# Two heads at a time in the dilated attention, and joined values in the mixer's

## The chip, the cores and the metric

The kernel runs on one core of a Trainium2 chip. Its metric is the device time of one execution in microseconds. TensorE (PE) multiplies, VectorE (DVE) and ScalarE (ACT) do the elementwise work, GpSimd (POOL) a few additions, and SyncE (SP) issues nearly all DMAs.

## What is computed

Two transformer blocks follow one another on 256 tokens of width 1024, in fp32. The first is FFN, a hybrid mixer (causal latent attention with 8 heads, and a gated convolution) and FFN. The second is a mixer of two attentions (branch A with 8 heads of 128, and branch B), an FFN and a gated embedding. The two places that matter here, cut down:

```python
def causal_mla_attention(...):            # mixer of block one, per head of 64 (+32 rotary)
    sc = (q_nope @ k_nope.T + q_rope @ k_rope.T) * scale      # 96 deep
    p = softmax(where(key <= query, sc, -inf))
    return p @ v                                              # 64 wide

def mixer_b(q, k, v, rel_bias):           # branch B of block two: 3 dilations x 4 heads of 64
    for g, (window, dilation) in enumerate(((128, 1), (512, 4), (2048, 16))):
        o, lse = dilated_group(...)       # banded softmax(q @ k.T + bias) @ v
    wts = softmax(stack(lses))            # over the three dilations
    return sum(wts * stack(outs))         # 4 heads of 64
```

## The kernel before

The activations lie transposed, features on partitions and tokens in the free dimension. A weight strip (256 columns of a matrix with 1024 rows) is loaded by SP into one of three `raw` buffers, ScalarE casts it to fp32r (`hi`), VectorE computes the rest (`lo`), and each product is three fp32r matmuls (lines 150 to 152): hi by hi, hi by lo, lo by hi. `gemm` runs 24 of them into half a bank of PSUM.

Attention is done in plain fp32. The generator `_stages` (line 38) works on the heads as a pipeline of three stages, which are called last stage first in each round: scores, then a turn (transposes of the probabilities on PE, and a copy out of PSUM by ScalarE), then values. `_interleave` (line 28) alternates these with steps of a projection. So the source has an order of its own, but each engine's order is fixed when the program is built and is not the source's: in the trace, later projections stand between steps that the source has closer together.

In the mixer of block one (from line 742) a head's scores are 96 rows deep. The values of an even head write partitions 0 to 63 of a bank `bo`, those of the odd head after it partitions 64 to 127, each two products (lines 774 and 776); after the odd one the bank is split into `oaH` and `oaL`. The projection work beside it is `gl`, later `y`.

In branch B (lines 1092 to 1137) an item is one head and one half of the queries, eight in all. The three dilations share one softmax over 512 columns: 256 keys of dilation 1, 128 each of dilations 4 and 16. Scores (line 1103) are three products over the 64 rows on which this head lies: partitions 0 to 63 or 64 to 127 of `qkB`. `bias_tile` (line 896) loads a bias tile from DRAM with two DMAs on SP, and GpSimd adds the masks to the near part, which `bias_near` has loaded once a head with four DMAs. VectorE adds the bias and takes the maximum (line 1108), ScalarE takes the exponential, VectorE scales by the reciprocal sum (line 1113). Four transposes follow (line 176), a copy (line 1121), and four products of values (line 1132) into the 64 partitions of `bob` that belong to the head. After two heads `bob` is copied, reordered and split. Beside it run the projection of branch A (`ya`, in `out_a`) and, after that, the gates (`gab`, `yb`, line 1183 on), whose `sg` takes a buffer of the tag `z`.

PSUM has two pools of four banks: `bankA` (scores, transposes, values) and `bankB` (projections).

Of the kernel before, what the change touches and what calls it, by code (L numbers as in the profile page):

```python
# [8 lines left out]
F32 = mybir.dt.float32  # L9
# [3 lines left out]
AF = mybir.ActivationFunctionType  # L13
ALU = mybir.AluOpType
# [13 lines left out]
def _interleave(a, b, na=1, nb=1):  # L28
    a, b = iter(a), iter(b)
    live_a = live_b = True  # L30
    while live_a or live_b:
        for _ in range(na):
            if live_a:
                try:
                    next(a)
                except StopIteration:
                    live_a = False
        for _ in range(nb):
            if live_b:
                try:  # L40
                    next(b)
                except StopIteration:
                    live_b = False


def _stages(n, stages, also):

    out = [None] * len(stages)
    for i in range(n + len(stages) - 1):
        if i in also:  # L50
            also[i]()
            yield
        new = list(out)
        for k in range(len(stages) - 1, -1, -1):
            if 0 <= i - k < n:
                new[k] = stages[k](*(out[k - 1] if k else (i,)))
                yield
        out = new
# [3 lines left out]
def tile_two_blocks(ctx: ExitStack, tc: tile.TileContext, t: dict, out: bass.AP):  # L62
# [11 lines left out]
    def bankA(name):  # L74
        return psA.tile([P, 512], F32, tag="acc", name=name)

    def bankB(name):
        return psB.tile([P, 512], F32, tag="ps", name=name)
# [4 lines left out]
    def tab(*args, **kw):  # L83
        if not last_table:
            last_table.append(act.activation(*args, **kw).ins)
        else:
            with tc.issue_after(last_table[0]):
                last_table[0] = act.activation(*args, **kw).ins  # L88
# [82 lines left out]
    def hilo(src, hi, lo):  # L171
        act.copy(hi, src)  # L172
        vec.tensor_tensor(out=lo, in0=src, in1=hi.bitcast(F32), op=ALU.subtract)  # L173

    def tr(dst, src, n=P):
        pe.transpose(out=dst, in_=src, identity=ident[:n, :n])
# [412 lines left out]
    def mixer_one(px, tmp2):  # L589
# [36 lines left out]
        def latent():  # L626
# [110 lines left out]
            o_attn.extend((oaH, oaL))  # L737
            scale = 96.0 ** -0.5
            regions = ((0, P), (P, 384))
            bo = {}  # L740

            def scores(hd):
                bs = bankA("bs")
# [17 lines left out]
            def turn_p(hd, sm):  # L761
                bt = bankA("bt")
                for i in range(3):
                    tr(bt[:, i * P:(i + 1) * P], sm[:, i * P:(i + 1) * P])
                pT = tmp2.tile([P, 384], F32, tag="pT", name="pT")
                act.copy(pT, bt[:, :384])
                return hd, pT

            def values(hd, pT):
                j = hd % 2  # L770
                if j == 0:
                    bo[0] = bankA("bo")
                o = bo[0][j * 64:j * 64 + 64, :]
                pe.matmul(o[:, 0:T], lhsT=vN[:, 0, hd * 64:hd * 64 + 64], rhs=pT[:, 0:T], start=True, stop=False,
                          skip_group_check=True)
                pe.matmul(o[:, P:T], lhsT=vN[:, 1, hd * 64:hd * 64 + 64], rhs=pT[:, T:384], start=False, stop=True,
                          skip_group_check=True)
                if j:
                    hilo(bo[0][:, :T], oaH[:, hd // 2, :], oaL[:, hd // 2, :])

            yield from _stages(8, (scores, turn_p, values), {2: lambda: (turn(nq, qT, "mq", 2), turn(nq, qT, "mq", 3))})

# [99 lines left out]

    def bias_near(px, j):

        stg = px.tile([P, 80], F32, tag="bias_s", name="bias_s", bufs=2)
        for rr in range(2):
            p0 = rr * 64

            for g, dst, su in ((1, stg[p0:p0 + 64, 0:64], (16 * 512 - 1, 512 - 4)),
                               (2, stg[p0:p0 + 64, 64:80], (16 * 512, 512 - 1))):  # L890
                row0 = ((4 * g + j) * P + p0) * 512
                sync.dma_start(out=dst, in_=bass.AP(bias_d.tensor, bias_d.offset + row0 + 256,
                                                    [[su[0], 4], [su[1], 16], [1, dst.shape[1]]]))
        return stg

    def bias_tile(px, j, qt, stg):

        bt = px.tile([P, 512], F32, tag="bias", name="bias", bufs=2)
        for rr in range(2):
            p0 = rr * 64  # L900
            row0 = (j * P + p0) * 512
            sync.dma_start(out=bt[p0:p0 + 64, 0:256],
                           in_=bass.AP(bias_d.tensor, bias_d.offset + row0 + 256 - 2 * qt - rr,
                                       [[16 * 512 - 4, 4], [512 - 16, 16], [1, 256]]))
        for m, a, n, o, so in ((m1, 2, 64, 256, 0), (m2, 8, 16, 384, 64)):
            pool.tensor_tensor(out=bt[:, o:o + P].rearrange("p (a b) -> p a b", a=a),
                               in0=m.rearrange("p (a b) -> p a b", a=a),
                               in1=stg[:, so:so + n].unsqueeze(1).to_broadcast([P, a, n]), op=ALU.add)
        return bt
# [5 lines left out]
    def mixer_two(px, tmp2):  # L915
# [17 lines left out]
        gg = tmp2.tile([P, 2, P], F32, tag="pT", name="gg")  # L933
        act.dma_start(out=gg[:, 0, :], in_=row_bc(t["q_norm_g_2"], P))
        act.dma_start(out=gg[:, 1, :], in_=row_bc(t["k_norm_g_2"], P))
        rtab = [px.tile([P, 2, 256], F32, tag="bias", name="rtab", bufs=2) for _ in range(2)]
        blk = lambda z: z.rearrange("p a (f s n) -> p a f s n", f=2, s=2)
        for i in range(2):
            g1 = gg[:, i:i + 1, :].to_broadcast([P, 2, P])
# [150 lines left out]
        bo_b, stage_b, ya = {}, {}, []  # L1090

        def scores_b(i):
            j, qt = divmod(i, 2)
            pr_, jj = divmod(j, 2)
            lo_, hi_ = jj * 64, jj * 64 + 64
            if qt == 0:
                stage_b[0] = bias_near(px, j)
            bias = bias_tile(px, j, qt, stage_b[0])
            bs = bankA("bs")
            qs = slice(qt * P, (qt + 1) * P)  # L1100
            for g in range(3):
                dst, ks = ((bs[:, 0:256], slice(0, T)), (bs[:, 256:384], qs), (bs[:, 384:512], qs))[g]
                pe.matmul(dst, lhsT=qB[lo_:hi_, 2 * g + pr_, qs], rhs=kB[lo_:hi_, 2 * g + pr_, ks], start=True, stop=True)
            sm = tmp2.tile([P, 512], F32, tag="sm", name="sm", bufs=3)
            mx = tmp.tile([P, 1], F32, tag="mx1", name="mx1")
            nb = tmp.tile([P, 1], F32, tag="nb1", name="nb1")
            se = tmp.tile([P, 1], F32, tag="se1", name="se1")
            vec.tensor_tensor_reduce(out=sm, in0=bs, in1=bias, scale=1.0, scalar=-3e38,
                                     op0=ALU.add, op1=ALU.max, accum_out=mx)
            vec.tensor_scalar_mul(nb, mx, -1.0)  # L1110
            tab(sm, sm, AF.Exp, bias=nb, accum_out=se)
            vec.reciprocal(se, se)
            vec.tensor_scalar_mul(sm, sm, se)
            return i, sm

        def turn_b(i, sm):
            bt = bankA("bt")
            for c in range(4):
                tr(bt[:, c * P:(c + 1) * P], sm[:, c * P:(c + 1) * P])
            pT = tmp2.tile([P, 512], F32, tag="pT", name="pT")  # L1120
            act.copy(pT, bt)
            return i, pT

        def values_b_of(i, pT):
            j, qt = divmod(i, 2)
            pr_, jj = divmod(j, 2)
            if i % 4 == 0:
                bo_b[0] = bankA("bob")
            bo = bo_b[0]
            for c in range(4):  # L1130
                v = vB[(0, 0, 1, 2)[c]][:, (0, 1, qt, qt)[c], j * 64:(j + 1) * 64]
                pe.matmul(bo[jj * 64:jj * 64 + 64, qt * P:(qt + 1) * P], lhsT=v, rhs=pT[:, c * P:(c + 1) * P],
                          start=c == 0, stop=c == 3, skip_group_check=True)
            if i % 4 == 3:
                fl = tmp.tile([P, T], F32, tag="nu", name="ob")
                act.copy(v16(fl), o16(bo[:, :T]))
                hilo(fl, obH[:, pr_, :], obL[:, pr_, :])

        def out_a():
            ya.append(px.tile([P, 8, T], F32, tag="qA", name="ya"))  # L1140
            for s in range(4):
                w = cols(t["w_out_a_2"][0], s * 256, 256)
                b = bankB("ya")
                for j in range(2):
                    gemm(b[:, j * T:(j + 1) * T], w, j * P, (oaH, oaL), KD)
                    yield
                vec.tensor_copy(flat(ya[0][:, 2 * s:2 * s + 2, :]), b)
# [22 lines left out]
                drain(q[0])  # L1170
        B = qkv_b()
        _interleave(chain(_stages(8, (scores_a, turn_a, values_a_of), {1: lambda: drain(q[1]), 3: lambda: drain(q[2]), 5: lambda: drain(q[3])})), B, 2, 1)
        _interleave(_stages(8, (scores_b, turn_b, values_b_of), {}), out_a())
        rb = rbs[0]
        wob = cols(t["w_out_b_2"][0], 0, 1024)
        mgH = px.tile([P, KD, T], F32R, tag="oAH", name="mgH2")
# [178 lines left out]
```

## Time and profile before

| | |
|---|---|
| median of 3 runs | 1050.9 us (1048.54 to 1056.88) |
| the profiled execution's own time | 1048.57 us |
| its span, first to last instruction | 1046.8 us |
| mean granted TensorE clock | 0.995 |
| PE busy | 1018.4 us (97%) |
| DVE busy | 741.7 us (71%) |
| ACT busy | 557.3 us (53%) |

Busy time is a share of the span; matmuls are pipelined, so the busy time of PE counts their overlaps once, and its rate is read from the distance between starts. PEld is the weight load of TensorE, which has rows of its own.

### The profile page before, as it was taken

How to read it: one execution, taken by the hardware profiler on the slowest of the kernel's cores; microseconds unless marked ns; L12 is line 12 of the kernel's file. 1: busy time of each engine (PE TensorE's matmuls, PEld its weight loads, DVE VectorE, ACT ScalarE, POOL GpSimd, SP SyncE). 2: the span in 40 equal slices, each digit the busy share in tenths (PEclk: the TensorE clock that was granted, in tenths of full speed). 3: DMA queues.
4: the chain of work that ended last, by engine and by line, in shares of the span. 5: the costliest groups of instructions: out<-in, count | busy, mean ns of one | idle time of the engine just before them, and what ended most of it. 6: DMA issues, size and time to landing. Idle time of an engine off the chain costs nothing.

```text
span 1046.8 us, 20303 instructions
## 1 busy us (share of the span) xinstructions
PE 1018.4 (97%) x8332; PEld 984.3 (94%) x8332; DVE 741.7 (71%) x1414; ACT 557.3 (53%) x1036; POOL 34.9 (3%) x47
## 2 busy tenths in 40 slices
PE   6999999999999999999999999999999999999996
PEld 3799999999989998999999999999899999999996
DVE  4789998657967998964545689656467776555565
ACT  5564554447656455643444555544456665445453
POOL 0000000010000011000000100001100100000010
PEclk9999999999999999999999999999999999999998
DMA  9899999425754987986554344445335885555311
GB/s 346 287 373 337 304 343 367 142 87 173 214 178 151 290 262 271 343 274 212 170 193 153 112 128 155 135 135 165 96 123 188 267 285 186 183 187 195 121 62 41
DMA packets 161301, 215.41 MB, mean 206 GB/s; under 512 B 6206, under 2 KB 129877, under 8 KB 161080
## 3 DMA queue, kind: packets, MB, share of 16 engines
q1 hardware_dynamic: 159346, 212.58, 61.4%
q10 hardware_dynamic: 1862, 1.53, 0.5%
q8 instruction: 65, 1.06, 0.4%
q14 instruction: 28, 0.23, 0.1%
HBM read 210.63 MB, written 3.47 MB: 205 GB/s over the span
## 4 chain that ended last, share of the span: by engine, by line
PE 82%; DVE 9%; ACT 3%; DMA 3%; issue 1%; POOL 0%; SPq 0%; DVEq 0%; ACTq 0%; POOLq 0%
PE gu L150 8%; PE gu L152 8%; PE gu L151 8%; PE acc L150 7%; PE acc L151 7%; PE acc L152 6%; DVE lo L140 3%; PE u L152 2%; PE u L150 2%; PE u L151 2%; PE gab L150 1%; DMA ada<-in_w_ada_dram 1%; ACT hi L139 1%; PE gab L152 1%; PE gab L151 1%
## 5 line engine op out<-in xcount | busy, mean ns | idle before, releaser
L140 DVE TENSOR_TENSOR lo<-raw,hi 128x512 fp32r<-128x512 f32 (+2 forms) x454 | 395.7, 903 | 102.9 <-ACT hi L139 101.7
L139 ACT CAST hi<-raw 128x512 fp32r<-128x512 f32 (+2 forms) x454 | 337.1, 786 | 222.3 <-PE acc L151 81.6
L150 PE MATMUL gu<-hh,hi 128*128 128x256 f32 x704 | 198.8, 283 | 0.0
L152 PE MATMUL gu<-hh,lo 128*128 128x256 f32 x704 | 197.6, 281 | 0.0
L151 PE MATMUL gu<-hl,hi 128*128 128x256 f32 x704 | 196.8, 280 | 0.0
L150 PE MATMUL acc<-mh,hi 128*128 128x256 f32 x608 | 170.2, 282 | 2.3 <-ACT mh L172 2.3
L151 PE MATMUL acc<-ml,hi 128*128 128x256 f32 x608 | 170.8, 281 | 0.0
L152 PE MATMUL acc<-mh,lo 128*128 128x256 f32 x608 | 170.2, 280 | 0.0
L151 PEld LDWEIGHTS gu<-hl,hi 128*128 128x128 f32 x704 | 133.0, 189 | 0.6 <-issue 0.5
L150 PEld LDWEIGHTS gu<-hh,hi 128*128 128x128 f32 x704 | 132.9, 189 | 0.6 <-issue 0.5
L152 PEld LDWEIGHTS gu<-hh,lo 128*128 128x128 f32 x704 | 132.8, 189 | 0.1
L150 PEld LDWEIGHTS acc<-mh,hi 128*128 128x128 f32 x608 | 114.0, 188 | 2.8 <-ACT mh L172 2.8
L151 PEld LDWEIGHTS acc<-ml,hi 128*128 128x128 f32 x608 | 114.5, 188 | 0.2 <-DVE ml L173 0.2
L152 PEld LDWEIGHTS acc<-mh,lo 128*128 128x128 f32 x608 | 114.7, 189 | 0.0
L267 DVE SCALAR_TENSOR_TENSOR ada_acc<-ada,c_act,ada_acc 128x512 f32<-128x512 f32 x98 | 73.6, 751 | 2.3 <-DMA ada<-in_w_ada_dram 0.6
L150 PE MATMUL u<-hh,hi 128*128 128x256 f32 x256 | 71.6, 280 | 0.0
L151 PE MATMUL u<-hl,hi 128*128 128x256 f32 x256 | 71.6, 280 | 0.0
L152 PE MATMUL u<-hh,lo 128*128 128x256 f32 x256 | 71.5, 279 | 0.0
L88 ACT ACTIVATE s<-gu 128x256 f32<-128x256 f32 x44 | 16.7, 382 | 75.2 <-PE gu L152 75.2
L331 POOL TENSOR_TENSOR ssum<-ssum,sq 128x256 f32<-128x256 f32 x25 | 23.3, 931 | 813.6 <-ACT sq L329 812.6
L151 PEld LDWEIGHTS u<-hl,hi 128*128 128x128 f32 x256 | 48.1, 188 | 0.2 <-DVE hl L376 0.2
L150 PEld LDWEIGHTS u<-hh,hi 128*128 128x128 f32 x256 | 48.1, 188 | 0.0
(379 smaller groups left out, 2221.9 us busy)
## 6 DMA issues: line engine op xcount, KB each, us to landing
raw<-in_ffn_w_dram SPq DMA_DIRECT2D x64, 1024.0 KB
raw<-in_w_in_dram SPq DMA_DIRECT2D x37, 1024.0 KB
raw<-in_w_ff_dram SPq DMA_DIRECT2D x32, 1024.0 KB
ada<-in_w_ada_dram SPq DMA_DIRECT2D x28, 1024.0 KB
raw<-in_w_out_dram SPq DMA_DIRECT2D x8, 1024.0 KB
ada<-in_w_ada_dram SPq DMA_DIRECT2D x8, 768.0 KB
raw<-in_w_branch_dram SPq DMA_DIRECT2D x8, 512.0 KB
raw<-in_w_out_a_dram SPq DMA_DIRECT2D x4, 1024.0 KB
```

The lines of the kernel that those rows point to most:

```text
L88: last_table[0] = act.activation(*args, **kw).ins
L139: act.copy(hi[:, sl], raw[:, sl])
L140: vec.tensor_tensor(out=lo[:, sl], in0=raw[:, sl], in1=hi[:, sl].bitcast(F32), op=ALU.subtract)
L150: pe.matmul(ps, lhsT=wh, rhs=xh, start=start, stop=False, skip_group_check=True)
L151: pe.matmul(ps, lhsT=wh, rhs=xl, start=False, stop=False, skip_group_check=True)
L152: pe.matmul(ps, lhsT=wl, rhs=xh, start=False, stop=stop, skip_group_check=True)
L267: vec.scalar_tensor_tensor(out=acc, in0=wv[:, k, :], scalar=c_act[:, k0 + k:k0 + k + 1], in1=acc, op0=ALU.mult, op1=ALU.add)
L331: pool.tensor_tensor(out=s[0], in0=s[0], in1=sq, op=ALU.add)
```

## The change

In branch B an item becomes a pair of heads and one half of the queries, four items in place of eight. The score products of the two heads alternate (head 0 on partitions 0 to 63, head 1 on 64 to 127), into two banks, as do their value products, into the two halves of one bank. Softmax is done head after head, as are the transposes and the copies. The second head's scores lie in a buffer of the tag `z`, its transposed ones in one of the tag `sq2`; `bob` moves to `bankB`. The bias tiles have three buffers, the near parts four.

In the mixer's attention, `values` of the even head only keeps its transposed probabilities; at the odd head the products of both alternate. Scores and transposes stay as they were, and `pT` has three buffers.

```diff
-                pT = tmp2.tile([P, 384], F32, tag="pT", name="pT")
+                pT = tmp2.tile([P, 384], F32, tag="pT", name="pT", bufs=3)
...
             def values(hd, pT):
-                j = hd % 2
-                if j == 0:
-                    bo[0] = bankA("bo")
-                o = bo[0][j * 64:j * 64 + 64, :]
-                pe.matmul(o[:, 0:T], lhsT=vN[:, 0, hd * 64:hd * 64 + 64], rhs=pT[:, 0:T], start=True, stop=False,
-                          skip_group_check=True)
-                pe.matmul(o[:, P:T], lhsT=vN[:, 1, hd * 64:hd * 64 + 64], rhs=pT[:, T:384], start=False, stop=True,
-                          skip_group_check=True)
-                if j:
-                    hilo(bo[0][:, :T], oaH[:, hd // 2, :], oaL[:, hd // 2, :])
+
+                pTs[hd % 2] = pT
+                if hd % 2 == 0:
+                    return
+                bo = bankA("bo")
+                for k, (a, e) in enumerate(((0, T), (T, 384))):
+                    for j in range(2):
+                        c = (hd - 1 + j) * 64
+                        pe.matmul(bo[j * 64:j * 64 + 64, k * P:T], lhsT=vN[:, k, c:c + 64], rhs=pTs[j][:, a:e],
+                                  start=k == 0, stop=k == 1, skip_group_check=True)
+                hilo(bo[:, :T], oaH[:, hd // 2, :], oaL[:, hd // 2, :])
...
-        stg = px.tile([P, 80], F32, tag="bias_s", name="bias_s", bufs=2)
+        stg = px.tile([P, 80], F32, tag="bias_s", name="bias_s", bufs=4)
...
-        bt = px.tile([P, 512], F32, tag="bias", name="bias", bufs=2)
+        bt = px.tile([P, 512], F32, tag="bias", name="bias", bufs=3)
...
         def scores_b(i):
...
+            pr_, qt = divmod(i, 2)
+            qs = slice(qt * P, (qt + 1) * P)
             if qt == 0:
-                stage_b[0] = bias_near(px, j)
...
+                stage_b.update({jj: bias_near(px, 2 * pr_ + jj) for jj in range(2)})
+            bias = [bias_tile(px, 2 * pr_ + jj, qt, stage_b[jj]) for jj in range(2)]
+            bs = [bankA("bs") for _ in range(2)]
             for g in range(3):
...
+                a, e, ks = ((0, 256, slice(0, T)), (256, 384, qs), (384, 512, qs))[g]
+                for jj in range(2):
+                    rows = slice(jj * 64, jj * 64 + 64)
+                    pe.matmul(bs[jj][:, a:e], lhsT=qB[rows, 2 * g + pr_, qs], rhs=kB[rows, 2 * g + pr_, ks], start=True, stop=True)
+            sms = []
+            for jj in range(2):
+                sm = tmp2.tile([P, 512], F32, **(dict(tag="sm", bufs=3) if jj == 0 else dict(tag="z")), name="sm")
...
+        def turn_b(i, sms):
+            pTs = []
+            for jj, sm in enumerate(sms):
+                bt = bankA("bt")
+                for c in range(4):
+                    tr(bt[:, c * P:(c + 1) * P], sm[:, c * P:(c + 1) * P])
+                pT = tmp2.tile([P, 512], F32, tag="pT" if jj == 0 else "sq2", name="pT")
+                act.copy(pT, bt)
+                pTs.append(pT)
+            return i, pTs
...
+        def values_b_of(i, pTs):
...
+            if qt == 0:
+                bo_b[0] = bankB("bob")
             bo = bo_b[0]
             for c in range(4):
...
+                for jj in range(2):
+                    j = 2 * pr_ + jj
+                    v = vB[(0, 0, 1, 2)[c]][:, (0, 1, qt, qt)[c], j * 64:(j + 1) * 64]
+                    pe.matmul(bo[jj * 64:jj * 64 + 64, qt * P:(qt + 1) * P], lhsT=v, rhs=pTs[jj][:, c * P:(c + 1) * P],
+                              start=c == 0, stop=c == 3, skip_group_check=True)
+            if qt == 1:
...
-        _interleave(_stages(8, (scores_b, turn_b, values_b_of), {}), out_a())
+        _interleave(_stages(4, (scores_b, turn_b, values_b_of), {}), out_a())
```

## Rows read from the trace of the kernel before

**Rows 1.** The page, parts 1 and 4: busy time of PE, chain that ended last.
```profile
PE 1018.4 (97%) x8332; PEld 984.3 (94%) x8332; DVE 741.7 (71%) x1414; ACT 557.3 (53%) x1036; POOL 34.9 (3%) x47
...
PE 82%; DVE 9%; ACT 3%; DMA 3%; issue 1%; POOL 0%; SPq 0%; DVEq 0%; ACTq 0%; POOLq 0%
```

**Rows 2.** Busy time of each engine (instructions), clock, DMA, in two stretches.
```profile
705.90:766.50 60.60, 60.42 (x463) 55.10 (x461) 33.35 (x75) 28.12 (x55) 7.79 (x12) 1.00 0.42 134
288.00:328.60 40.60, 40.60 (x301) 36.15 (x299) 26.31 (x83) 24.27 (x57) 0.00 (x0) 1.00 0.51 159
```

**Rows 3.** Timeline of PE, branch B, one head's scores: start, length, instructions merged.
```profile
714.16 0.28 PE L152 MATMUL ya<-oAH,lo 128*128 128x256 f32 x1
714.37 1.14 PE L1103 MATMUL bs<-qkB 64*128 64x256 f32 x6
...
715.66 0.28 PE L151 MATMUL ya<-oAL,hi 128*128 128x256 f32 x1
```

**Rows 4.** Timeline of PE, branch B, one head's values.
```profile
718.23 0.27 PE L152 MATMUL ya<-oAH,lo 128*128 128x256 f32 x1
718.43 1.09 PE L1132 MATMUL bob<-pT,vB 128*64 128x128 f32 x8
...
719.68 0.28 PE L151 MATMUL ya<-oAL,hi 128*128 128x256 f32 x1
```

**Rows 5.** Timeline of PE, branch B, one head's transposes.
```profile
722.37 0.60 PE L176 MATMUL bt<-ident,sm 128*128 128x128 f32 x4
...
722.92 0.28 PE L151 MATMUL ya<-oAL,hi 128*128 128x256 f32 x1
```

**Rows 6.** Timeline of PE, branch A, four full-array fp32 instructions of 256 columns.
```profile
659.38 1.02 PE L1006 MATMUL bs<-kA,qA 128*128 128x256 f32 x4
```

**Rows 7.** Timeline of PE, branch B, scores with values straight behind.
```profile
736.85 0.28 PE L152 MATMUL ya<-oAH,lo 128*128 128x256 f32 x1
737.05 1.14 PE L1103 MATMUL bs<-qkB 64*128 64x256 f32 x6
738.12 1.09 PE L1132 MATMUL bob<-pT,vB 128*64 128x128 f32 x8
...
739.36 0.28 PE L151 MATMUL gab<-hl,hi 128*128 128x256 f32 x1
```

**Rows 8.** Timeline of PE, the mixer of block one, one head's values.
```profile
298.75 0.28 PE L151 MATMUL gl<-hl,hi 128*128 128x256 f32 x1
298.96 0.65 PE L774 MATMUL bo<-pT,vN 128*64 128x256 f32 x2
...
299.98 0.28 PE L150 MATMUL gl<-hh,hi 128*128 128x256 f32 x1
```

**Rows 9.** Weight loads by tile, branch B: durations in ns (least/median/most).
```profile
L1103 PEld LDWEIGHTS bs<-qkB x48: 182/187/188, 706.0 to 758.2; 64*128 64x128 f32 x48
```
```profile
L1132 PEld LDWEIGHTS bob<-pT,vB x64: 132/137/137, 718.4 to 766.2; 128*64 128x64 f32 x64
```

**Rows 10.** Timeline of the weight loads that belong to the values of rows 4.
```profile
718.43 0.85 PEld L1132 LDWEIGHTS bob<-pT,vB 128*64 128x64 f32 x8
```

**Rows 11.** Timeline of VectorE, branch B, one softmax and weight splits after it.
```profile
726.98 0.69 DVE L1108 CUSTOM_DVE_ANT_0 sm<-bs,bias 128x512 f32<-128x512 f32 x1 [1.01 <-issue]
...
728.95 0.49 DVE L1113 TENSOR_SCALAR sm<-sm,se 128x512 f32<-128x512 f32 x1
...
730.49 2.49 DVE L140 TENSOR_TENSOR lo<-raw,hi 128x512 fp32r<-128x512 f32 x4
```

**Rows 12.** Timeline of PE, branch B: scores, and the transposes of the same head.
```profile
748.66 1.14 PE L1103 MATMUL bs<-qkB 64*128 64x256 f32 x6
...
752.50 0.60 PE L176 MATMUL bt<-ident,sm 128*128 128x128 f32 x4
```

**Rows 13.** PE by line, 705 to 767 us: busy, mean ns, idle before.
```profile
L176 PE MATMUL bt<-ident,sm 128*128 128x128 f32 x32 | 4.9, 277 | 0.2
```

**Rows 14.** Timeline of SP's DMA issues, branch B.
```profile
718.19 2.13 SPq L892 DMA_DIRECT2D bias_s<-bias_d  x4
720.43 5.94 SPq L125 DMA_DIRECT2D raw<-in_w_in_dram  x2
```

More of the change, by code (lines that the diff above doesn't have):

```diff
@@ L739, in latent @@
             regions = ((0, P), (P, 384))
-            bo = {}
+            pTs = {}
             def scores(hd):
@@ L935, in mixer_two @@
         act.dma_start(out=gg[:, 1, :], in_=row_bc(t["k_norm_g_2"], P))
-        rtab = [px.tile([P, 2, 256], F32, tag="bias", name="rtab", bufs=2) for _ in range(2)]
+        rtab = [px.tile([P, 2, 256], F32, tag="bias", name="rtab", bufs=3) for _ in range(2)]
         blk = lambda z: z.rearrange("p a (f s n) -> p a f s n", f=2, s=2)
@@ L1092, in scores_b @@
         def scores_b(i):
-            j, qt = divmod(i, 2)
-            pr_, jj = divmod(j, 2)
-            lo_, hi_ = jj * 64, jj * 64 + 64
+            pr_, qt = divmod(i, 2)
+            qs = slice(qt * P, (qt + 1) * P)
             if qt == 0:
-                stage_b[0] = bias_near(px, j)
-            bias = bias_tile(px, j, qt, stage_b[0])
-            bs = bankA("bs")
-            qs = slice(qt * P, (qt + 1) * P)
+                stage_b.update({jj: bias_near(px, 2 * pr_ + jj) for jj in range(2)})
@@ L1101, in scores_b @@
+            bias = [bias_tile(px, 2 * pr_ + jj, qt, stage_b[jj]) for jj in range(2)]
+            bs = [bankA("bs") for _ in range(2)]
             for g in range(3):
[L1102 to L1128, printed above, removed]
+                a, e, ks = ((0, 256, slice(0, T)), (256, 384, qs), (384, 512, qs))[g]
@@ new lines, in scores_b @@
+                for jj in range(2):
[4 more added lines that the diff above has]
+                sm = tmp2.tile([P, 512], F32, **(dict(tag="sm", bufs=3) if jj == 0 else dict(tag="z")), name="sm")
+                mx = tmp.tile([P, 1], F32, tag="mx1", name="mx1")
+                nb = tmp.tile([P, 1], F32, tag="nb1", name="nb1")
+                se = tmp.tile([P, 1], F32, tag="se1", name="se1")
+                vec.tensor_tensor_reduce(out=sm, in0=bs[jj], in1=bias[jj], scale=1.0, scalar=-3e38,
+                                         op0=ALU.add, op1=ALU.max, accum_out=mx)
+                vec.tensor_scalar_mul(nb, mx, -1.0)
+                tab(sm, sm, AF.Exp, bias=nb, accum_out=se)
+                vec.reciprocal(se, se)
+                vec.tensor_scalar_mul(sm, sm, se)
+                sms.append(sm)
@@ new lines, in scores_b @@
+            return i, sms
+        def turn_b(i, sms):
[9 more added lines that the diff above has]
+        def values_b_of(i, pTs):
+            pr_, qt = divmod(i, 2)
+            if qt == 0:
+                bo_b[0] = bankB("bob")
@@ L1129, in values_b_of @@
             bo = bo_b[0]
             for c in range(4):
[L1131 to L1134, printed above, removed]
+                for jj in range(2):
[3 more added lines that the diff above has]
+                              start=c == 0, stop=c == 3, skip_group_check=True)
```

## The prediction

> **What bounds the kernel now.** I read the page first: TensorE is busy 97% of the span and holds 82% of the chain that ended last [rows 1]. Then the busy time by stretch for the two places that the diff touches: branch B's attention (705.9 to 766.5 us) and the mixer's attention (288.0 to 328.6). In both PE is busy nearly without a break at granted clock 1.00, VectorE and ScalarE for about half to two thirds of the time [rows 2]. So time comes off only where TensorE needs less of it, provided that nothing opens a hole in its stream. A busy PE doesn't say how fast it goes, so next I read the timeline of PE, for the distance from one start to the next.
>
> An fp32r matmul of the projections follows its neighbour after 0.117 us (22 steps from 715.66 to 718.23 [rows 3, 4]). An fp32 matmul shows as two instructions. Full-array fp32 transposes cost only their own streams: 722.37 to 722.92 is 0.55 us, four transposes of 0.11 and one step of 0.117 [rows 5]. An fp32 instruction of 256 columns takes (1.02 - 0.38)/3 = 0.215 us [rows 6].
>
> The narrow matmuls cost more than their streams:
> - Scores of one head in branch B (64 rows of the array): 714.16 to 715.66 less 0.23 is 1.27 us [rows 3]. The streams are 2 x 0.215 + 4 x 0.11 = 0.87; the other 0.40 is spent in crossing into the half array and back.
> - Values of one head (64 columns): 718.23 to 719.68 less 0.23 is 1.22 us [rows 4], streams 8 x 0.11 = 0.87, crossings 0.35.
> - Scores followed directly by values: 736.85 to 739.36 less 0.23 is 2.28 us [rows 7], streams 1.74, three crossings 0.54.
> - Values of one head of the mixer: 298.75 to 299.98 less 0.23 is 1.00 us [rows 8], streams 0.65, crossings 0.35.
>
> **The change, part by part.** No multiplication is added or dropped: the numbers of matmuls, transposes, reductions, exponentials and copies stay. Only their grouping changes, and which half of the array stands next to which.
>
> *Fewer crossings in branch B.* The timeline of the stage has five blocks of scores that stand alone (the first head's is cut in two), four of values alone and four of both: 5 x 0.40 + 4 x 0.35 + 4 x 0.54 = 5.6 us. With two heads at a time there are four blocks of each: 3.0 us if none adjoin, 2.2 if all do; I take 2.6, half way. Saved: **3.0** (2.6 to 3.4).
>
> *Two heads' scores side by side.* Head 0 sits on partitions 0 to 63, head 1 on 64 to 127, and they now alternate, into two banks. Nothing in the trace of before runs two heads at once, so I bound it. Upper end of the cost: every change of half is a crossing like those into a mode now, 0.40/2 = 0.20 us; five changes inside a pair, 4 x (1.74 + 1.0) = 11.0 us, a loss of 4.0. No overlap and no crossing: 8 x 0.87 = 7.0 us as now. Lower end: an instruction runs beside the one of the other half next to it. Since each fp32 matmul is two instructions of the same half, and they start in program order, the pattern is first | second beside the other half's first | ..., so a pair takes 3 x 0.215 + 4 x 0.11 = 1.08 us. Weights may bind sooner: a load of 128 columns lasts 187 ns, one of 64 lasts 137 [rows 9], so 128 columns are about 0.10 us, and twelve loads one after another 1.2 us. I take 1.18 us x 4 = 4.7. Saved: **2.2** (-4.0 to 2.6). I take the overlapped end because already in one head's block a load runs under the matmul before it, at the pace of the streams: eight loads of values in 0.85 us, their matmuls in 1.09 [rows 4, 10].
>
> *Two heads' values side by side.* Same reasoning in columns: 16 instructions in nine steps of 0.11 us, 0.98 us for a pair, 3.9 in all, against 8 x 0.87 = 7.0. Saved: **3.0** (3.5 at most; with a crossing of 0.35/2 at each of seven changes a loss of 4.9).
>
> *The mixer's values.* Even heads wait one step for the odd one, on a third pT buffer. Eight blocks become four: crossings 4 x 0.35 = **1.4** saved. Streams 8 x 0.65 = 5.2 become 4 x (3 x 0.215 + 2 x 0.11) = 3.5: **1.7** saved (2.0 at most; with three crossings a loss of 2.1). ScalarE's copies of pT stay where they are, and the joined result was split only after the odd head before, too.
>
> *What is moved, and its cover.* Softmax of two heads now stands between a pair's scores and its transposes. One head's chain on VectorE and ScalarE lasts 726.98 to 729.44, 2.5 us [rows 11]; the second adds about 0.7 to 1.5. PE's first transpose waits for head 0, the fifth for head 1, and every projection matmul queued behind them on PE waits too. The cover is the ya and gab projections: of 5.6 us for a strip, they already stand between scores and transposes, which come 3.8 to 8.0 us after (748.66 to 752.50; 714.37 to 722.37) [rows 3, 5, 12]. PE was idle before branch B's transposes for 0.2 us in the whole stage [rows 13]. I charge **0.6** us (0.15 a step; 0 to 15 as bounds; the upper end is rival 4). Bias tiles: two per step out of three slots in place of one out of two, and eight near-diagonal loads at once, 4.3 us on SP in place of 2.1; the weight loads behind them on SP have slack, since SP issues one of them only every 5 us or more (two in 5.94) [rows 14] and three strips are buffered. Without that cover it would cost those 2.1 us once. sg of the gates shares its two slots with the second heads' scores, and bob moves to the other four banks; two gab banks ahead (11 us of PE) cover both. Nothing for these.
>
> *Sum.* 3.0 + 2.2 + 3.0 + 1.4 + 1.7 = 11.3, less 0.6: **10.7 us**, all on PE's own path. The profiled execution took 1048.57 us (span 1046.8), so it would take 1037.9. That execution is at the lowest of the three runs (1048.54); their median, 1050.9, is 2.3 higher, so a median of after lies between 1037.9 and 1040.2. I put down **1038.5**.
>
> **The rivals.**
> 1. *The halves don't run side by side*: the change regroups, but fp32 instructions of two halves still follow one another. For it: nowhere in the trace do two matmuls of different halves overlap, and fp32 already needs two instructions. Against: the loads do overlap with running matmuls [rows 10]. Then only crossings are saved: 3.0 + 1.4 - 0.6 = 3.8, 1044.8 us.
> 2. *Only the row halves overlap.* If a load cannot slip under a matmul that occupies the same rows, the column pairs (all of whose weights lie on the same 128 rows) stay serial: 3.0 + 2.2 + 1.4 - 0.6 = 6.0, 1042.6 us. Against: the loads of values run under values' matmuls today, all on the same rows [rows 10]. The same section of the Trainium skill says that loads overlap with matmuls in flight only when the row groups differ; by that rule it is this rival. The trace speaks against a plain reading of it.
> 3. *Every change of half drains the array* (slower side). Alternating makes 5 + 7 + 3 = 15 changes in one pair of each kind, 60 in all. If each costs a crossing as it does today on the way into and out of a half, 0.175 to 0.20 us [rows 3, 4, 8], that is 4.0 + 4.9 + 2.1 = 11.0 us against the 3.8 of rival 1: 1055.8 us. It decides from 3.8/60 = 0.063 us per change. For it: all narrow work of before pays at its edges, and none of it shows a change of half without a change of shape. Against: what costs today is a change of the shape in use (full, half rows, half columns), and the halves of one shape need nothing reset that the trace shows. The Trainium skill, page "TensorEngine Tiling (Array Packing)", section "Tiling Modes", says that changing the mode drains TensorE and changing only the tile doesn't; by that rule this rival falls.
> 4. *PE waits for the paired softmax* (slower side as well). Between scores and transposes the source puts one ya product, 2.8 us. The chain of two heads is 3.2 to 4.0 us alone, and 5.7 to 6.5 behind a run of four weight splits on VectorE (2.49 us) [rows 11]. If PE's order kept to the source, each of four steps would idle 0.4 to 3.7 us, at most 15 us against 11.3: 1052 us; with bias tiles that come late by as much again, 1067. It decides from 2.8 us of idle per step. Against it: today's order isn't the source's; 8.0 us lie between scores and transposes where the source has one product of 2.8 [rows 3, 5], and PE's idle time before transposes is 0.2 us in all [rows 13].
>
> **How the numbers follow.** Side by side in both: 0.53. Rival 1: 0.21. Rival 2 (or the mirror of it, rows serial and columns not): 0.12. Rivals 3 and 4: 0.07 each. Range: the low end is all upper savings without waits, 3.4 + 2.6 + 3.5 + 1.4 + 2.0 = 12.9, so 1035.7, put at 1035.5; the high end takes in rival 1, most of it with the 2.3 us by which a median may lie higher: 1046.5. Rivals 3 and 4 are left out. The measurement of this kernel can tell about 1% from no change, 10.5 us: below 1040.4 counts as faster. The forecast lies close to that edge: three quarters of its 0.53 fall below, and a little of rival 2: 0.42. Over 1061.4 is rival 4 with late bias tiles, and rival 3 if its changes cost a little more than today's: 0.04. The rest, 0.54, is within 1%.
>
> **What would show it.** PE's timeline of the changed kernel: a scores block of 12 instructions lasting about 1.2 + 0.40 us between projections (2.1 if serial); a values block of 16 about 1.0 + 0.35 (2.1 if serial); in the mixer, 8 instructions in about 0.87 + 0.35 (1.65 if serial); starts of the two halves within a few hundredths of each other; for rival 3, gaps of 0.2 us inside a block. Branch B's attention, 705.9 to 766.5 now, should hold as many projection matmuls per us as elsewhere. Idle time of PE before the transposes should stay under 1 us; over 3 us a step makes me wrong on the slow side, as would PE waiting for sg or a bias tile. If the blocks shrink and the end doesn't move, another resource took over after all.

## The result, and the profile after

| | before | after |
|---|---|---|
| first comparison, median | 1053.72 us (4 runs, 1048.54 to 1056.88) | 1040.07 us (4 runs, 1039.59 to 1041.59) |
| ratio, 95% interval | | 0.9898 (0.987 to 0.9926) |
| once more, later, median | 1049.14 us (10 runs) | 1040.49 us (5 runs) |
| ratio, 95% interval | | 0.9924 (0.9912 to 0.9937) |
| profiled execution (span) | 1048.57 us (1046.8) | 1039.59 us (1037.8) |

The changed kernel is faster by 0.8 to 1.0%, about 9 us, where 10.7 were forecast (1048.57 to 1037.9). The two medians of the kernel before differ by 4.6 us, those of the changed one by 0.4, so the second ratio is the better one. (The ratios are those on record; the quotients of the medians are 0.987 and 0.992.) The gain is real and lies at the 1% that I took as the limit of what can be told: of the changed kernel's two medians one falls just below my edge of 1040.4 us, the other just above.

The page of the changed kernel, parts 1 and 4, answers to [rows 1]: TensorE lost 8.5 us of busy time, and no other engine took over the end.

```profile
PE 1009.9 (97%) x8332; PEld 977.6 (94%) x8332; DVE 741.2 (71%) x1414; ACT 557.7 (54%) x1036; POOL 34.4 (3%) x47
...
PE 88%; DVE 7%; ACT 3%; DMA 1%; issue 1%; POOL 0%; ACTq 0%; DVEq 0%; POOLq 0%; SPq 0%
```

**Where the time went.** The attention of [rows 2] is interleaved with projections, so I cut the trace where the work in between is the same. For branch B that is from the last `vb` matmul to the first `u` matmul; for the mixer, from the first `bs` matmul to the last `y` matmul. Busy time by stretch (length; busy us and instructions of PE, PEld, DVE, ACT and POOL; granted clock; share and GB/s of DMA, as in [rows 2]), the kernel before:

```profile
705.80:826.62 120.82, 120.57 (x967) 114.51 (x966) 82.05 (x168) 66.64 (x135) 12.63 (x17) 1.00 0.49 155
...
288.00:374.82 86.82, 86.00 (x698) 81.09 (x696) 70.32 (x147) 50.64 (x93) 0.00 (x0) 1.00 0.68 213
```

and the changed one:

```profile
706.00:818.05 112.05, 111.14 (x967) 107.16 (x966) 80.86 (x168) 66.81 (x135) 10.48 (x15) 1.00 0.53 165
...
287.20:373.90 86.70, 85.19 (x698) 79.72 (x696) 69.61 (x146) 49.61 (x92) 0.00 (x0) 1.00 0.69 222
```

The counts of matmuls agree (967 and 698), so each pair is the same work. Branch B's stretch is 8.8 us shorter, the mixer's 0.1 us. The whole gain is branch B's; of the mixer's 3.1 us nothing has come.

**How two heads run.** PE's timeline of branch B after the change (start, length, instructions merged) answers to [rows 3] and [rows 4]:

```profile
715.43 0.28 PE L152 MATMUL ya<-oAH,lo 128*128 128x256 f32 x1
715.64 1.15 PE L1105 MATMUL bs<-qkB 64*128 64x256 f32 x12
...
716.94 0.28 PE L151 MATMUL ya<-oAL,hi 128*128 128x256 f32 x1
...
719.51 0.27 PE L152 MATMUL ya<-oAH,lo 128*128 128x256 f32 x1
719.71 1.09 PE L1142 MATMUL bob<-pT,vB 128*64 128x128 f32 x16
...
720.97 0.28 PE L151 MATMUL ya<-oAL,hi 128*128 128x256 f32 x1
```

Twelve score instructions take 715.43 to 716.94 less 0.23 (two steps of 0.117), 1.28 us; six of them took 1.27. Sixteen for the values take 719.51 to 720.97 less 0.23, 1.23 us; eight took 1.22. A second head costs 0.01 us. The instructions under way in each slice of that score block (its own line alone) say how:

```profile
715.60:715.75 0.15, 0.11 (x2) 0.11 (x3) 1.00 1.08 341
715.75:715.95 0.20, 0.20 (x2) 0.19 (x4) 1.00 1.13 358
```

Both heads are under way in the first 0.15 us (x2). By the records (the starts of single instructions in the trace) the two halves start 7 ns apart (715.638 and 715.645; 715.958 and 715.965), through the whole block. My picture of instructions that start in program order, each matmul's two one after the other, was too careful: the first instruction of one half runs beside the first of the other, the second beside the second.

The loads run side by side too. The weight loads of the sixteen value instructions take as long as the eight of [rows 10]:

```profile
719.71 0.85 PEld L1142 LDWEIGHTS bob<-pT,vB 128*64 128x64 f32 x16
```

### The profile page after: what moved, and what is told of

Read it like the earlier page. It is cut to its first block, busy times and chain, and to the rows that moved or that the text cites. A ratio compares the mean times of both kernels' runs of the same rounds, so it can differ in the third digit from the quotient of the medians.

```text
span 1037.8 us, 20288 instructions
## 1 busy us (share of the span) xinstructions
PE 1009.9 (97%) x8332; PEld 977.6 (94%) x8332; DVE 741.2 (71%) x1414; ACT 557.7 (54%) x1036; POOL 34.4 (3%) x47
## 3 DMA queue, kind: packets, MB, share of 16 engines
q8 instruction: 65, 1.06, 0.4%
## 4 chain that ended last, share of the span: by engine, by line
PE 88%; DVE 7%; ACT 3%; DMA 1%; issue 1%; POOL 0%; ACTq 0%; DVEq 0%; POOLq 0%; SPq 0%
PE gu L150 8%; PE gu L152 8%; PE gu L151 8%; PE acc L150 7%; PE acc L151 7%; PE acc L152 7%; PE u L152 2%; PE u L150 2%; PE u L151 2%; DVE lo L140 1%; PE po L150 1%; PE po L151 1%; PE gab L152 1%; PE po L152 1%; PE gab L150 1%; PE gab L151 1%
```

## The experiments

Each run stands beside runs of the kernel before on the same chip (medians 1049.1 to 1049.6 us). Edits are to the changed kernel unless the text says otherwise.

**1. Either half of the change alone.** The first kernel has the changed branch B and the mixer of before; the second has the joined mixer and branch B of before.

```diff
 # b_only, on the changed kernel
-                pTs[hd % 2] = pT
-                if hd % 2 == 0:
-                    return
...
+                pe.matmul(o[:, 0:T], lhsT=vN[:, 0, hd * 64:hd * 64 + 64], rhs=pT[:, 0:T], start=True, stop=False,
+                          skip_group_check=True)
 # mixer_only: the same lines the other way, on the kernel before
```

> Branch B as changed, the mixer's values as before. Theory: the whole gain is branch B's, where two heads cost as much of TensorE as one did; the mixer's joining gives at most 0.2 us. Then this is 8.5 to 9 us faster than the kernel before, and within 1 us of the changed kernel. Rival, my own sum: the mixer's joining is worth 3.1 us, and this is about 3 us slower than the changed kernel.

> The mixer's values joined as changed, branch B as before. Theory: no more than 0.5 us faster than the kernel before, because three of the four joined blocks are cut in two by projection matmuls and TensorE waits before transposes. Rival, my own sum: 3.1 us faster. Second rival: TensorE needs 3 us less in the mixer's attention, but the stretch up to the next FFN takes them back; then the last projection of the mixer ends 3 us earlier and the end stays.

Branch B alone: 1041.76 us (6 runs), ratio 0.9921 (0.9907 to 0.9935). The mixer alone: 1049.42 us (12 runs), 0.9996 (0.9988 to 1.0004). The stretch of branch B in the first kernel:

```profile
708.10:820.75 112.65, 111.79 (x967) 107.83 (x966) 80.84 (x168) 66.67 (x135) 10.49 (x15) 1.00 0.52 165
```

That is 8.2 us less than before, and about as much comes off the time (0.9921 of 1049.6 is 8.3 us less; by medians it is 7.8); in the second kernel the stretch is as long as before (last `vb` at 707.31, first `u` at 828.30, 121.0 us). The mixer's part gives nothing that twelve runs can tell.

**2. Does the order of issue matter?** Both kernels have the whole change, with branch B's products in another order: head after head (three score products, then three; four value products, then four), and values in runs of two.

```diff
 # b_grouped (values likewise)
-            for g in range(3):
-                a, e, ks = ((0, 256, slice(0, T)), (256, 384, qs), (384, 512, qs))[g]
-                for jj in range(2):
+            for jj in range(2):
+                for g in range(3):
+                    a, e, ks = ((0, 256, slice(0, T)), (256, 384, qs), (384, 512, qs))[g]
 # b_runs2
-            for c in range(4):
-                for jj in range(2):
+            for c0 in (0, 2):
+                for jj, c in ((0, c0), (0, c0 + 1), (1, c0), (1, c0 + 1)):
```

> The changed kernel, but in branch B the products of a pair are listed head after head instead of in turn: six of the fp32 score products as A A A B B B, eight of the values as A A A A B B B B. Theory: two halves run side by side only when they alternate in the instruction stream, so this gives back nearly all of the overlapped streams, 4 x (0.87 + 0.87) = 7.0 us less one overlapped step in each block (8 x 0.11 = 0.9): 6 us slower than the changed kernel, and still 3 us faster than the kernel before, by the crossings. Rival: TensorE finds the other half's work further down its queue, and the order doesn't matter: the time of the changed kernel.

> The changed kernel, but branch B's value products come in runs of two, A A B B A A B B; scores still alternate. Theory from the run with grouped heads: the other half's product may start while one product of the first half is running and one more is queued, so runs of two still run side by side: values of a pair take the 0.93 us of the changed kernel, within 0.1, and the time is the changed kernel's within 1 us. Rival: only neighbours overlap, so a run of two loses about half of what runs of four lose: 0.25 us or more in each block, 1 us in all.

Head after head: 1043.32 us (4 runs), ratio 0.9938 (0.9923 to 0.9953). Runs of two: 1040.55 us (4 runs), 0.9916 (0.9902 to 0.9931). The first is 3 us slower than the changed kernel, not the 6 of my theory and not the nothing of the rival. PE's timeline of it:

```profile
716.34 0.27 PE L152 MATMUL ya<-oAH,lo 128*128 128x256 f32 x1
716.54 1.68 PE L1105 MATMUL bs<-qkB 64*128 64x256 f32 x12
...
718.38 0.28 PE L151 MATMUL ya<-oAL,hi 128*128 128x256 f32 x1
...
720.94 0.28 PE L152 MATMUL ya<-oAH,lo 128*128 128x256 f32 x1
721.15 1.58 PE L1142 MATMUL bob<-pT,vB 128*64 128x128 f32 x16
...
722.88 0.28 PE L151 MATMUL ya<-oAL,hi 128*128 128x256 f32 x1
```

and its value instructions under way in two slices:

```profile
721.10:721.63 0.53, 0.48 (x4) 0.49 (x5) 1.00 0.27 97
721.63:721.80 0.17, 0.17 (x6) 0.17 (x5) 1.00 0.30 102
```

The blocks cost 1.81 and 1.71 us in place of 1.28 and 1.23; fully serial they would cost 1.74 + 0.40 and 1.74 + 0.35 (2.14 and 2.09). For 0.5 us the first head runs alone (x4, two of its four value products), then both together (x6 in 0.17 us). By the records the second head starts 6 ns after the start of the first head's third value product, and 6 ns after that of its second score product: in both cases when one product of the first head is left that hasn't started. In runs of two only one such product stands ahead of the other head; by the records both heads then start 13 ns apart, and the block is back at 1.27 us (721.38 to 722.88 less 0.23). Counted in instructions, two to a product, the second head starts as soon as three of the first head's are still waiting ahead of it, and doesn't while four are. This takes PE's program to have the products in the order of the source, which the trace doesn't show by itself; in all three kernels the starts fit that order. PE's timeline:

```profile
721.38 0.27 PE L152 MATMUL ya<-oAH,lo 128*128 128x256 f32 x1
721.58 1.14 PE L1142 MATMUL bob<-pT,vB 128*64 128x128 f32 x16
...
722.88 0.28 PE L151 MATMUL ya<-oAL,hi 128*128 128x256 f32 x1
```

So here it is enough to alternate so closely that no more than one waiting product of the same half stands ahead. The changed kernel's strict alternation satisfies that.

**3. Why the mixer gives nothing.** PE's timeline of the changed kernel's mixer shows two things:

```profile
306.34 0.60 PE L745 MATMUL bs<-kT,qT 96*128 96x256 f32 x2
306.87 0.65 PE L778 MATMUL bo<-pT,vN 128*64 128x256 f32 x2
...
307.79 0.28 PE L150 MATMUL gl<-hh,hi 128*128 128x256 f32 x1
308.00 0.86 PE L778 MATMUL bo<-pT,vN 128*64 128x256 f32 x6
...
309.01 0.28 PE L152 MATMUL gl<-hh,lo 128*128 128x256 f32 x1
...
323.92 0.27 PE L152 MATMUL gl<-hh,lo 128*128 128x256 f32 x1
325.33 0.33 PE L176 MATMUL bt<-ident,sm 128*128 128x128 f32 x1 [1.14 <-DVE sm L758]
```

First, three of the four joined blocks are cut: the even head's first product (x2) goes ahead alone, since its pT is ready and the odd head's isn't, and projections fill the time. The rest (x6) then costs 307.79 to 309.01 less 0.23, 0.99 us, on top of about 0.8 for the cut-off piece: 1.8 in place of the 2.0 of two single heads [rows 8]. The fourth, the first in time, is whole but has the score block straight in front (297.78), and costs 1.2 us. So the four blocks save 1.6 us, not 3.1. Second, PE stands still before the last head's transposes. PE by line, 284 to 345 us, first before, then after:

```profile
L176 PE MATMUL bt<-ident,sm 128*128 128x128 f32 x24 | 5.2, 274 | 0.0
```
```profile
L176 PE MATMUL bt<-ident,sm 128*128 128x128 f32 x24 | 5.5, 284 | 1.5 <-DVE sm L758 1.1 <-ACT qT L722 0.2
```

Before, the values of head 6 stood at this place (323.59 in the trace) and with `gl` projections covered head 7's softmax. Now they wait for head 7, the 192 `gl` matmuls that serve as filling are used up sooner (the last starts at 323.92), and 1.14 us are idle here, 1.5 before all transposes. By the records, from start to start, the gaps at the transposes grow by 2.3 us in all, which is more than the blocks save. That the stretch isn't longer than before comes from a wait of 0.8 us for ScalarE further on (`ada_b`), which the kernel before has and the changed one hasn't; why it goes, no run isolates. PE's timeline before:

```profile
357.37 0.18 PE L277 MATMUL ada_ps<-one,ada_b 128*128 128x1 bf16 x1 [0.82 <-ACT ada_b L271]
```

Two kernels try this: the odd head's product is issued first (so that no piece can go ahead), and besides that heads 6 and 7 are left single.

```diff
 # late_first
-                    for j in range(2):
+                    for j in (1, 0):
 # tail_single, on top of it: heads 6 and 7 each at their own turn
-                if hd % 2 == 0:
-                    return
+                if hd >= 6:
+                    jobs = ((hd % 2, 0), (hd % 2, 1))
+                elif hd % 2:
+                    jobs = ((1, 0), (0, 0), (1, 1), (0, 1))
+                else:
+                    return
```

> The changed kernel, but in the mixer's joined values the odd head's product comes first in each pair. Its transposed probabilities arrive last, so nothing of the block can start ahead of it, and the block isn't cut in two. Theory: four whole blocks of 0.65 + 0.35 us in place of three cut ones and a staggered one; each cut costs about 0.9 us, so the mixer's attention is 2 to 3 us shorter and the kernel 2 us faster than the changed one. Rival: what the mixer's attention saves is taken back before the next FFN (clock, norm), and the time doesn't move.

> As the kernel with the odd head first, but the mixer's last two heads keep single values, so that head 6's products stand between the last scores and the last transposes again. Theory: the joined mixer loses because work that covered the last softmax is moved behind it; TensorE's idle time ahead of the last transposes falls from 1.1 us to 0.3 or less, and the stretch from the first scores to the last y product before 345 us, 51.7 us with all heads joined, falls to 50.7 or less. Rival: the projections of the gates run out whatever the values do, and the stretch stays at 51.4 or more. The end of the kernel moves by under 1 us either way if what lies between the mixer's attention and the next FFN takes it back.

The odd head first: 1040.02 us (6 runs), ratio 0.991 (0.9892 to 0.9928), not to be told from the changed kernel, where my theory had 2 us. PE's timeline:

```profile
316.54 0.28 PE L152 MATMUL gl<-hh,lo 128*128 128x256 f32 x1
316.75 0.87 PE L778 MATMUL bo<-pT,vN 128*64 128x256 f32 x8
...
317.77 0.28 PE L151 MATMUL gl<-hl,hi 128*128 128x256 f32 x1
...
323.81 0.70 PE L176 MATMUL bt<-ident,sm 128*128 128x128 f32 x3 [1.14 <-DVE sm L758]
325.56 1.55 PE L778 MATMUL bo<-pT,vN 128*64 128x256 f32 x8 [1.06 <-ACT pT L766]
327.04 0.58 PE L150 MATMUL y<-ocH,hi 128*128 128x256 f32 x1
```

and the stretches around it, where clock is the last column but two:

```profile
325.00:326.90 1.90, 1.34 (x8) 0.77 (x8) 1.79 (x4) 1.90 (x4) 0.00 (x0) 0.57 0.00 0
327.00:328.60 1.60, 1.60 (x9) 1.56 (x8) 1.60 (x4) 1.31 (x2) 0.00 (x0) 0.50 0.92 229
328.70:331.00 2.30, 2.30 (x21) 2.30 (x21) 1.17 (x2) 0.00 (x0) 0.00 (x0) 1.00 0.65 167
```

The first three blocks are whole now (x8), and each costs 1.00 us (316.54 to 317.77 less 0.23) in place of 2.00. But the last pair has nothing left beside it: 1.14 us of waiting for the softmax, 1.06 more for the copy of pT, and in the second of these holes the granted clock falls to its lower level, 0.50 (1.2 GHz), and stays there for 3.4 us (by the records 325.25 to 328.66). `y`'s matmuls there start 0.21 us apart (327.42 to 328.49) in place of 0.117. The blocks' saving went into this, all but 0.2 us by the last `y` (from the first `bs`, start to start, 86.75 us before and 86.51 here).

With heads 6 and 7 single: 1038.03 us (5 runs), 0.9889 (0.9875 to 0.9904). Because that is the fastest of all, it ran again beside the changed kernel:

> The changed kernel once more, beside its variant with heads 6 and 7 single in the mixer, on one chip. Theory (branch B gives nearly all, the mixer nothing): 0.991 of the kernel before, branch B's stage 112 us, PE idle for over 1 us before the mixer's last bt transposes. Rival (the 0.9898 of the first result had a part from the mixer): 0.990 here, and level with the variant.

> Changed kernel with the odd head's product first and heads 6 and 7 single. Theory (the covered softmax is worth under 2 us, and the stretch after the mixer takes most of it back): 0.989 to 0.991 of the kernel before, at most 2 us below the changed kernel beside it. Rival (the 2.4 us that the mixer's stage lost less in this variant reach the end): 0.9885 or less, and over 2 us below the changed kernel.

The changed kernel: 1040.49 us (5 runs), 0.9924 (0.9912 to 0.9937); the variant: 1038.09 us (4 runs), 0.9892 (0.9877 to 0.9907). The intervals don't meet; the two edits together are worth 2.4 us, a little over the 2 of my theory, and the first of them alone was worth none. The second trace of the changed kernel repeats the first: 112.1 us for branch B, 86.6 for the mixer, 1.1 idle before the last transposes. The variant's stretch from the first `bs` to the last `y`, and the end of its mixer:

```profile
287.15:371.62 84.47, 83.79 (x699) 79.78 (x697) 68.53 (x145) 49.01 (x91) 0.00 (x0) 1.00 0.69 217
```
```profile
323.69 0.30 PE L176 MATMUL bt<-ident,sm 128*128 128x128 f32 x1 [0.24 <-DVE sm L758]
...
325.54 0.86 PE L783 MATMUL bo<-pT,vN 128*64 128x256 f32 x4
```

The stretch is 2.35 us shorter than before (86.82 to 84.47). By the records three joined blocks save 3.1 us, the gaps at the transposes grow by 1.3 us in all (0.6 of it shows as idle time), and the wait for `ada_b` is down by 0.7: 3.1 - 1.3 + 0.7 = 2.5 us.

**4. Does the stretch pass a saving on?** In the kernel before, one value product of each head in the mixer is left out, or done twice.

```diff
 # mixer_less: this product goes; mixer_more: it stands twice
                 pe.matmul(o[:, P:T], lhsT=vN[:, 1, hd * 64:hd * 64 + 64], rhs=pT[:, T:384], start=False, stop=True,
                           skip_group_check=True)
```

> The kernel before, without the second value product of each head in the mixer (keys 128 to 255 are left out), so TensorE needs 8 x 0.22 = 1.8 us less in that attention. Theory: time that TensorE saves there is not passed on, because each odd step already waits for a softmax of 2.9 us and the stretch to the next FFN is paced by VectorE and DMA: at most 0.5 us faster than the kernel before. Rival, my prediction's assumption: all of it is passed on, 1.8 us faster.

> The kernel before, with the second value product of each head in the mixer done twice (keys 128 to 255 count double), 1.8 us more of TensorE in that attention. Theory: the following stretch, paced by VectorE and DMA, takes some of it back: 0 to 1 us slower than the kernel before. Rival: TensorE sets the time there, 1.8 us slower.

Less work: 1049.49 us (11 runs), ratio 1.0004 (0.9995 to 1.0012). More work: 1049.52 us (12 runs), 0.9998 (0.9986 to 1.001). 1.8 us of TensorE off or on (16 instructions of 0.11) move the end by nothing that can be measured; the intervals leave room for 0.5 us less and 1.0 us more. In the traces the stretch from the first `bs` to the last `y` (86.75 us before, start to start) is 1.2 us shorter with less work and 1.0 longer with more. One place that takes less work back is the same hole, PE by line of that kernel, 284 to 345 us:

```profile
L176 PE MATMUL bt<-ident,sm 128*128 128x128 f32 x24 | 5.4, 277 | 1.1 <-DVE sm L758 1.1
```

The kernel before has no such hole (0.0 above), so it isn't that its odd steps already waited, as I had put it; the wait arises when work goes. With more work, the wait of 0.8 us for `ada_b` is gone, which leaves 1.0 of the 1.8.

A second place where time may go lies behind the mixer, in front of the FFN: a norm, 24 `bias_ps` matmuls and the first `gu`. PE's timeline and the busy time of one stretch, of the kernel before and then of the changed one:

```profile
397.92 0.28 PE L152 MATMUL po<-mg,lo 128*128 128x256 f32 x1
...
401.27 4.56 PE L877 MATMUL bias_ps<-hot,tabs 33*128 33x512 f32 x22
405.76 0.97 PE L150 MATMUL gu<-hh,hi 128*128 128x256 f32 x2
```
```profile
396.00:412.00 16.00, 15.88 (x99) 12.50 (x99) 13.52 (x25) 9.32 (x20) 2.09 (x2) 0.89 0.82 290
```
```profile
396.94 0.28 PE L152 MATMUL po<-mg,lo 128*128 128x256 f32 x1
...
400.09 5.38 PE L878 MATMUL bias_ps<-hot,tabs 33*128 33x512 f32 x22
405.40 0.79 PE L150 MATMUL gu<-hh,hi 128*128 128x256 f32 x2
```
```profile
396.00:412.00 16.00, 16.00 (x90) 12.97 (x89) 13.13 (x28) 9.86 (x21) 0.60 (x1) 0.79 0.87 308
```

In both PE is busy nearly throughout (15.88 and 16.00 of the 16 us, so the trace doesn't show VectorE and DMA setting the pace, as I had put it), and the granted clock falls to its lower level (0.50, 1.2 GHz) as these few thin matmuls run: in the kernel before with the last of them, for 3.4 us (by the records 405.66 to 409.08), in the changed one in their midst, for 6.8 us (403.59 to 410.42). The changed kernel comes to this place 0.98 us sooner (396.94 for 397.92), is granted 0.79 in place of 0.89 over the 16 us, its `bias_ps` take 5.38 us in place of 4.56, and `gu` starts only 0.36 us sooner. The mean is 0.79 with less work in the mixer too, and 0.89 with more work.

That the early arrival is the cause isn't shown. The kernel of run 1 with the joined mixer alone has the changed kernel's mixer, but its `bias_ps` take 4.54 us and its clock is low for 3.4 us; the changed kernel's second trace arrives at 400.15, later than before, and has 4.99 and 6.8 us. Of the twelve traces four have 3.4 us at the lower level (26.7 to 27.0 us from the last `po` to the 101st `gu`), seven have 6.8 (27.9 to 28.0 us), one has 13.7. So an execution can lose 1 us here, and those of the changed kernel and of the one with less work did, but single executions don't settle how often that is, or whether a saving brings it about; I didn't vary this stretch by itself. The variant's 2.4 us did reach the end.

## Why the prediction was nearly right, and where it wasn't

The forecast was 1038.5 us, the range 1035.5 to 1046.5; both medians (1040.07, 1040.49) lie within it. The mechanism was the forecast one, two halves side by side, but the terms were off in both directions:

| term | forecast | measured |
|---|---|---|
| branch B, crossings | 3.0 | about 2.1 |
| branch B, scores side by side | 2.2 | 3.5 |
| branch B, values side by side | 3.0 | 3.5 |
| branch B, waits before transposes | -0.6 | about -0.4 |
| branch B in all | 7.6 | 8.8 (stretch) |
| the mixer | 3.1 | 0.1 (stretch) |

- *Scores and values side by side* were sized too small. I let program order stagger the instructions and the weight loads follow one another (1.18 us for a pair of scores, 0.98 for a pair of values). Both pairs take the 0.87 us of one head's streams: 4 x 0.87 saved in each. For the scores that is more than the 2.6 that I had as the best case.
- *Crossings.* The blocks still pay what I read from [rows 3, 4, 7] at their edges: 1.28 - 0.87 and 1.23 - 0.87. But the first scores block and the last values block are cut in two (706.18 and 707.91; 745.85 and 746.76 in the timeline), and only one pair adjoins. Four scores blocks alone, four values blocks alone and one of both come to 4 x 0.40 + 4 x 0.35 + 0.54 = 3.5 us where I took 2.6; 5.6 - 3.5 = 2.1.
- *Waits for the paired softmax* are 0.6 us in branch B (before 0.2), most of it before the transposes at 744.54. The ya and gab projections cover the second head's chain as forecast, so rival 4 falls.
- *The mixer* is the step that failed, and it is 3.1 us of the 10.7. I counted matmul time saved on a stretch in which PE was busy without a break [rows 2], and named no cover for the work that moves: that head 6's values had been hiding head 7's softmax, and that the filling (`gl`) has a fixed amount. I had also taken it that a joined block stays joined. Runs 1, 3 and 4 show what came in place of this: the mixer alone gives nothing, a cut block saves about 0.25 us of the 0.78 that I had counted for a pair (a whole one saves 1.0), and time taken off PE there turns into waits before the transposes (1.5 us idle, of it 1.14 before the last).
- *Rivals 1 and 2* fall. Both halves overlap, rows and columns alike. The Trainium skill, page "TensorE: Matmul & The Clock Gate", section "Part 3: Packing small matmuls — row/col tiling" (the section that rival 2 leaves unnamed), lets weight loads overlap with matmuls in flight only when the row groups differ; the two column halves here share all rows, and their loads and matmuls ran at full overlap (sixteen loads in 0.85 us), so the measurement decides against that reading. The same section's model for packed tiles (one matmul's duration and about 4 ns for each further tile) fits, with 7 ns in place of 4.
- *Rival 3* falls: the changes of half, 48 in branch B, cost nothing that the timeline shows (starts within a half are 0.11 and 0.21 us apart behind the first, those of the streams), while the change of shape at the block's edges still costs 0.17 to 0.20 us. That agrees with what the page "TensorEngine Tiling (Array Packing)", section "Tiling Modes", of the Trainium skill says of modes and tiles.

That the forecast came out near is partly luck, since the errors cancelled in part: branch B gave 1.2 us more than forecast, the mixer 3.0 less. The profiled execution fell by 9.0 us (1048.57 to 1039.59), 8.8 of it in branch B's stretch; the rest of the trace differs by amounts that differ as much between executions of the same code (from the first `bs` to the mixer's last `po` 109.9 us before and 111.7 in the kernel with branch B alone; 109.7 and 112.4 in the two traces of the changed kernel).

## What to carry to other kernels

Two half-array matmuls of different halves, issued alternately into separate outputs, cost here what one costs, in fp32 and in row halves as in column halves; look for pairs wherever a timeline shows half-array work between full-array work, and keep at most one product of the same half waiting ahead of the other's. Before you join work across steps, ask what the early half was covering where it stood: at the end of a pipeline, with the filling used up, leave the last steps single. And read a saving off a stretch of the same work from end to end, and check in it which waits came and went, since time saved on a busy engine may come back as idle time a few us later.

## What I had not expected of the hardware

- The second half is free to 0.01 us per block: starts 7 ns apart, weight loads included.
- TensorE finds the other half's product behind one waiting product of the first half, not behind two; in instructions, behind three, not behind four (block 1.71 us for AAAABBBB, 1.27 for AABBAABB, 1.23 for ABABABAB).
- In the kernel with the odd head first, the granted clock fell to 0.50 in the second of two idle holes (1.14 and 1.06 us within 3 us) and stayed there for 3.4 us, then rose to 1.00. In the changed kernel, with the first hole alone, it stayed at 1.00.
- At the thin stretch before the FFN the time at the lower clock differs between executions of the same code: with the joined mixer 22 `bias_ps` matmuls took 4.54 us and the clock was low for 3.4 us in one trace, 5.38 and 4.99 us, with 6.8 us low, in the two of the changed kernel.
